# Dense products moved between the visits and the waits of a head pair, and the first attention head's loads in two queues

## The chip, the cores and the metric

The kernel runs on one core of a Trainium2 chip. The metric is the device time of one execution in microseconds, given as the median of repeated runs. Beside it stands one profiled execution, from which all durations below are read. The engines are called TensorE (PE in the rows, its weight loads PEld), VectorE (DVE), ScalarE (ACT), GpSimd (POOL) and SyncE (SP); ACTq and SPq are the queues from which ScalarE and SyncE start transfers.

## What is computed

One layer of a hybrid model over 128 prompt tokens and 512 latent tokens, T = 640 in all, of width 1024. It mixes differential attention (4 heads) with a bidirectional RWKV-7 scan (8 heads of 64), gates the two, and ends in a convolutional gated MLP. The outputs are both token groups, the new keys and values and the final scan states.

```python
h = x * (1 + sc1) + sh1
proj = h @ p['w_in']
q, k, v, rw, gates = jnp.split(proj, [...])          # 3 * 512 | 1792 | 2048 columns
o_att = diff_attention(apply_rope(q), [apply_rope(k), k_ctx], [v, v_ctx], lam)   # latents; the prompt has no rotary
# RWKV, for both directions d, token after token:
sa = jnp.einsum('bhvk,bhk->bhv', S, a_t)
S = S * w_t[:, :, None, :] + sa[..., None] * b_t[:, :, None, :] + v_t[..., None] * k_t[:, :, None, :]
y = jnp.einsum('bhvk,bhk->bhv', S, r_t)
...
o_rw = (y_rw * g_rw) @ p['w_o_rwkv']
mix = (ga * (o_att @ p['w_o_attn']) + gb * o_rw) @ p['w_out']
x = layer_norm(ALPHA * x + g1 * mix, ...)
# then ConvGLU: w_up, a 3-tap convolution, gelu(u) * val, w_down, a second layer norm
```

## The kernel before

Everything keeps features on the 128 partitions and tokens along the free axis, in two halves of 320 (HALF). The program runs in stages: modulation and the first input columns (up to some 70 us), the mixer (to 687 us), the attention (to about 787 us), the output projections and the MLP. The change lies in the mixer and at the first head of the attention.

**Dense products.** All columns of `w_in` are computed by `dense_steps` (L215): for each of 8 blocks of the inner dimension and each half of the tokens, three matrix products (high part by high part, high by low, low by high) in one PSUM bank. `load_w` brings a slab of four weight blocks in (L183, SyncE's queue), casts it on ScalarE (L186, `wh`) and subtracts on GpSimd (L187, `wl`). There are three buffers each for `ws`, `wh` and `wl`. A finished half is evacuated by ScalarE: into `raw` for the RWKV columns, into `vt` at L937 for the values, into `tg` at L1009 for the gates.

**The flow.** These products, with the work of `rw_a` (the RWKV projections of a head pair), `values`, `qk_head` and `gate`, form one long generator, `flow`. `pull(n)` takes its next n products and writes them into the program at the place of the call; `need(i, key)` pulls until a named input of pair i is there. `behind(n, f)` puts a function f after the next n products of the flow: the transposes of the values (L944) and of the keys (L981, L982) stand behind 14. TensorE's order is the order in which the program is written here, so each `pull(n)` fixes how many dense products stand at its place.

**A head pair.** The eight RWKV heads go in four pairs, i = 0 to 3. The recurrence is done in 10 chunks of 64 tokens for each of the two directions. The steps of a pair:

- `rw_c` (L644) multiplies AR by BK for all chunks; VectorE masks the results into MS (L651).
- `rw_i` inverts the 32 x 32 triangles on VectorE: four transposes (L704), each followed by `side()` and `pull(8)`; then 30 rounds of substitution (L711 to L713), each with `pull(4)`; then two transposes into Y11 (L722), four back into MS, and `pull(56)`. Beside it run generators kept in `sides`: `rw_d` (transposes of BK and values) and, for i > 0, `rw_f(i - 1)`, the normalization and gating of the pair before (L888 to L914), whose last instruction stores `yr`.
- `rw_m` completes the inverse in two small multiplications (L735, L743) with an evacuation between them by ScalarE (L737, `Vt`) and a `pull(12)`. Then come ten **visits**, v = 0 to 9. A visit has, as far as it exists, four transposes of a group of chunks (`turned`, L766), `joined` of the group before (L802 to L820), `solved` of its own group (L781), a sequential `step` of the states (L828, L830), then `side(3)` and `pull(10)`. The results of `solved` are copied to QQ (L788) and UV (L793) by VectorE and ScalarE; the next visit's `joined` reads them at L802 and L805. In the visits of pairs 0 to 2 the side generator is `rw_b(i + 1)`, which prepares the next pair's AR, BK and decays on VectorE and GpSimd.
- `rw_e` reads out the outputs (L869, evacuated by ScalarE at L870) and transposes the final states (L876).

The main loop (L1025 to L1047) goes through the pairs: `rw_e(i - 1)`, `need(i, "v_in")`, `rw_c(i)`, `rw_i(i)`, `rw_m(i)`. After `rw_f(3)` the rest of the flow is pulled without a pause.

**The attention's first head.** `load_head` (L1083 to L1094) brings queries and keys of one head from `qk_dram` with twelve transfers (L1090), then the values. `attend` starts with the scores (L1109). The loads of head 0 are written after the mixer, but the scheduler places them on SyncE's queue among the last of the mixer's transfers.

Of the kernel before, what the change touches and what calls it, by code (L numbers as in the profile page):

```python
# [11 lines left out]
F32 = mybir.dt.float32  # L12
# [54 lines left out]
def tile_layer(ctx, tc, x_prompt, x_sample, cache_k, cache_v, state_rwkv, c, c_ctx, w_ada, b_ada, w_in,  # L67
# [4 lines left out]
    nc = tc.nc  # L72
# [364 lines left out]
    def behind(n, f):  # L437

        later.append([n, f])
# [257 lines left out]
    def rw_i(i):  # L697
        MS = R[i]["MS"]

        X = rp.tile([P, 32, 32], F32, name="X", tag="st")  # L700
        tmp = rp.tile([P, 256], F32, name="tmpx", tag="tmpx")
        turns = [(X[32 * g:32 * g + 32], MS[32 * (g // 2):32 * (g // 2) + 32, 8 * (g % 2):8 * (g % 2) + 32, 32 * (g // 2):32 * (g // 2) + 32].rearrange("p c t -> p t c")) for g in range(4)]
        for x, m in turns:
            nc.vector.transpose(out=x, in_=m)  # L704
            side()
            pull(8)
        nc.vector.memset(X.rearrange("p t s -> p (t s)")[:, ::33], 1.0)
        for j in range(1, 31):
            n = 31 - j
            tv = tmp[:, 0:j * n].rearrange("p (t r) -> p t r", r=j)  # L710
            nc.vector.tensor_tensor(out=tv, in0=X[:, j:j + 1, 0:j].broadcast_to([P, n, j]),  # L711
                                    in1=X[:, j + 1:32, j:j + 1].broadcast_to([P, n, j]), op=ALU.mult)
            nc.vector.tensor_tensor(out=X[:, j + 1:32, 0:j], in0=X[:, j + 1:32, 0:j], in1=tv, op=ALU.add)  # L713
            side()
            pull(4)
        while "d_in" not in R[i]:
            side()
            pull(4)

        Y11 = rp.tile([32, 32, 40], F32, name="Y11", tag="bk", bufs=2)  # L720
        for g in range(2):
            nc.vector.transpose(out=Y11[:, :, 8 * g:8 * g + 32], in_=X[32 * g:32 * g + 32].rearrange("p t s -> p s t"))  # L722
        R[i].update(Y11=Y11)
        for x, m in turns[2:] + turns[:2]:
            nc.vector.transpose(out=m, in_=x)
        pull(56)

    def rw_m(i):
        AR, BT, UV, gs, st_in, MS = (R[i][k] for k in ("AR", "BT", "UV", "gs", "st_in", "MS"))
# [6 lines left out]
        for g in range(4):  # L736
            nc.scalar.copy(  # L737
                out=Vt[32:64, g::4, :], in_=ps[32 * g:32 * g + 32, 0:320].rearrange("p (c s) -> p c s", s=32))
        pull(12)
        ps = bank(psR, "m", 2)  # L740
        for ix in range(40):
            g, sl = ix % 4, ix // 4
# [89 lines left out]
        for v in range(10):  # L832
            put = turned(v + 1) if 0 < v < 4 else None
            if v == 0:
                turned(0)()
                pull(10)
                put = turned(1)
            if 1 <= v <= 5:
                joined(v - 1)
            if v < 5:  # L840
                solved(v)
            if put:
                put()
            if v > 2:
                s = v - 3
                step([(d, cc, ST[:, d, cc + 1 - 2 * d, :]) for d, cc in ((0, 2 + s), (1, 9 - s))] +
                     ([(0, 1, FS[0]), (1, 0, FS[1])] if v == 7 else []))
            side(3)
            pull(10)
        R[i].update(UV=UV, ST=ST, FS=FS)  # L850

    def rw_e(i):
# [79 lines left out]
    def values(n4):  # L932
        vt = fl.tile([P, T], F32, name="vt", tag="o", bufs=OB)
        new = newx()

        def evac(cols, pd, bias):
            nc.scalar.activation(out=vt[:, cols], in_=pd, func=AF.Identity, bias=bias)  # L937

        def turned():
            vs = fl.tile([P, 5, P], F32, name="vs", tag="o", bufs=OB)  # L940
            for z0, nz in ((0, 4), (4, 1)):
                ps = new()
                for z in range(nz):
                    pq(nc.tensor.transpose(out=ps[:, z * P:(z + 1) * P], in_=vt[:, (z0 + z) * P:(z0 + z + 1) * P], identity=ident))  # L944
                nc.vector.tensor_copy(out=vs[:, z0:z0 + nz, :], in_=ps[:, 0:nz * P].rearrange("p (b n) -> p b n", n=P))
            AQ.dma_start(out=v_dram[n4].rearrange("b p n -> p b n"), in_=vs)
            AQ.dma_start(out=new_v[:, n4 * P:(n4 + 1) * P], in_=vs[:, 0, :])

        yield from project_in(load_w(w_in[:, 1024 + n4 * P:1024 + (n4 + 1) * P], KB), evac, new=new)
        behind(14, turned)  # L950

    def qk(h, col, out, scale, new):
        w = load_w(w_in[:, col:col + P], KB)
# [48 lines left out]
    qk_dram = tc.dram_tile([2, 4, 2, P, T + P], F32, name="qk_dram")  # L1002
# [22 lines left out]
    for i in range(4):  # L1025
        if i:
            rw_e(i - 1)
        else:
            pull(40)
        need(i, "v_in")  # L1030
        sides.append(rw_d(i))
        rw_c(i)
        if i:
            sides.append(rw_f(i - 1))
        rw_i(i)
        if i < 3:
            need(i + 1, "rk_in")
            sides.append(rw_b(i + 1))
        else:
            pull(10)  # L1040
        rw_m(i)
        while sides:
            side()
            pull(3)
# [38 lines left out]
    def load_head(h):  # L1083
        qs, kh, kl = [], [], []
        for m in range(2):
            rows = slice(64 * m, 64 * m + 64)
            for lst, nm, w, z, ys, nb in ((qs, "qs", T, 0, (0, 1), QSB), (kh, "ks", T + P, 1, (0, 0), 2 * QSB), (kl, "ks", T + P, 1, (1, 1), 2 * QSB)):
                t_ = ap_.tile([P, w], F32R, name=nm, tag=nm, bufs=nb)
                for y in range(2):
                    nc.sync.dma_start(out=t_[64 * y:64 * y + 64, :].bitcast(F32), in_=qk_dram[z, h, ys[y], rows, 0:w])  # L1090
                lst.append(t_)
        V = ap_.tile([P, 6, P], F32, name="V", tag="V", bufs=2)
        nc.sync.dma_start(out=V[:, 0:5, :], in_=v_dram[h].rearrange("b p n -> p b n"))
# [514 lines left out]
```

## Time and profile before

| | |
|---|---|
| median of 3 runs | 1409.14 us (1409.0 to 1413.62) |
| profiled execution, its own time | 1415.6 us |
| span of the profiled execution | 1413.6 us |
| TensorE busy | 1254.3 us, 89% of the span |
| VectorE busy | 960.7 us, 68% |
| GpSimd, ScalarE busy | 553.4 and 544.0 us, 39% and 38% |
| mean granted clock of TensorE | 0.941 of full speed |
| moved by DMA | 144.57 MB, mean 102 GB/s |

How the rows of the trace are read. In the page's list of groups a row names line, engine, operation, output and inputs and the number of instructions; behind the first bar stand their busy time in us and the mean of one in ns, behind the second the engine's idle time before them and what ended most of it. In the busy time by stretches, a row gives the stretch (us from the start of the span) and its length, the busy time of each engine with the number of instructions in brackets, then the granted clock of TensorE (1.00 is 2.4 GHz, 0.50 is 1.2 GHz), the busy share of the DMA engines and the GB/s moved; a share over 1 means that more transfers were under way than there are engines. In the order of time, a row gives start, duration, engine, line, operation, output and inputs, the number of consecutive instructions merged in the row, and in square brackets how long the engine was idle before it and what it had waited for.

### The profile page before, as it was taken

The page shows a single profiled execution, that of the slowest core. Times are in us where ns is not written, and L with a number is a line of the kernel's source. Part 1 is how long each engine was busy: PE and PEld are TensorE (multiplying, and loading weights), DVE is VectorE, ACT ScalarE, POOL GpSimd, SP SyncE. Part 2 cuts the span into 40 slices and gives each one's busy share as a digit, 9 for nine tenths or more (in the row PEclk, how much of TensorE's full clock was granted, in tenths as well). Part 3 has the DMA queues.
Part 4 walks back from the last instruction along what each step waited for, and adds up shares of the span by engine and source line. Part 5 has one row for each costly group of instructions (what it writes and reads, how often), then busy time and mean ns, then how long its engine had stood idle before and what let it go on. Part 6 is the DMA issues. An engine that isn't in the chain of part 4 may idle for free. (4 is left out here: it accounts for less than half of the span.)

```text
span 1413.6 us, 26568 instructions
## 1 busy us (share of the span) xinstructions
PE 1254.3 (89%) x10583; PEld 1118.5 (79%) x10583; DVE 960.7 (68%) x1672; ACT 544.0 (38%) x1122; POOL 553.4 (39%) x415
## 2 busy tenths in 40 slices
PE   6989878887879899999888989969999999999995
PEld 5888777786768788889777777758988988989984
DVE  2367948896868667931366433687997987768778
ACT  3444333333333334232355321464443433434440
POOL 2244225432542232212220244546644635635631
PEclk9989979988998899989889999999999999999998
DMA  9412112221221111212666888423232231322222
GB/s 308 129 41 65 53 58 61 65 75 54 63 72 61 50 34 51 85 50 76 189 183 216 267 259 266 136 72 93 81 106 68 75 97 58 99 69 76 75 75 82
DMA packets 157455, 144.57 MB, mean 102 GB/s; under 512 B 10490, under 2 KB 128020, under 8 KB 157332
## 3 DMA queue, kind: packets, MB, share of 16 engines
q1 hardware_dynamic: 147490, 127.85, 29.6%
q10 hardware_dynamic: 9842, 15.03, 3.1%
q8 instruction: 83, 1.36, 0.4%
q14 instruction: 40, 0.33, 0.1%
HBM read 121.06 MB, written 19.69 MB: 100 GB/s over the span
## 5 line engine op out<-in xcount | busy, mean ns | idle before, releaser
L187 POOL TENSOR_TENSOR wl<-ws,wh 128x512 fp32r<-128x512 f32 x100 | 139.1, 1393 | 393.2 <-ACT wh L186 361.6
L224 POOL TENSOR_TENSOR wl<-sums,wh 128x512 fp32r<-128x512 f32 x88 | 137.0, 1562 | 39.4 <-ACT wh L223 35.7
L1431 PE MATMUL ps_d<-oph,wh 128*128 128x320 f32 x440 | 137.6, 313 | 11.6 <-DVE u L1443 5.2
L224 POOL TENSOR_TENSOR wl<-wu,wh 128x512 fp32r<-128x512 f32 x63 | 88.8, 1409 | 142.6 <-ACT wh L223 129.2
L1431 PE MATMUL ps_d<-oph,wl 128*128 128x320 f32 x440 | 137.0, 311 | 1.2 <-POOL wl L224 1.2
L1431 PE MATMUL ps_d<-opl,wh 128*128 128x320 f32 x440 | 136.5, 310 | 1.1 <-DVE opl L224 1.1
L186 ACT CAST wh<-ws 128x512 fp32r<-128x512 f32 x100 | 61.6, 618 | 136.7 <-PE ps_d L215 37.2
L215 PE MATMUL ps_d<-hh,wl 128*128 128x320 f32 (+1 forms) x304 | 102.8, 338 | 0.0
L215 PE MATMUL ps_x<-hh,wl 128*128 128x320 f32 (+1 forms) x304 | 101.6, 334 | 0.6 <-POOL wl L187 0.6
L215 PE MATMUL ps_d<-hl,wh 128*128 128x320 f32 (+1 forms) x304 | 102.0, 335 | 0.0
L215 PE MATMUL ps_x<-hh,wh 128*128 128x320 f32 (+1 forms) x304 | 101.8, 335 | 0.0
L215 PE MATMUL ps_d<-hh,wh 128*128 128x320 f32 (+1 forms) x304 | 101.6, 334 | 0.0
L215 PE MATMUL ps_x<-hl,wh 128*128 128x320 f32 (+1 forms) x304 | 101.2, 333 | 0.0
L1431 PEld LDWEIGHTS ps_d<-oph,wh 128*128 128x128 f32 x440 | 83.0, 189 | 16.0 <-ACT wh L223 9.1
L1431 PEld LDWEIGHTS ps_d<-opl,wh 128*128 128x128 f32 x440 | 83.0, 189 | 2.3 <-POOL hf L1346 1.3
L1431 PEld LDWEIGHTS ps_d<-oph,wl 128*128 128x128 f32 x440 | 83.1, 189 | 1.9 <-POOL wl L224 1.7
L223 ACT CAST wh<-sums 128x512 fp32r<-128x512 f32 x88 | 54.6, 620 | 64.7 <-PE ps_e L1431 25.2
L1465 PE MATMUL acc<-wh,gh 128*128 128x512 f32 x185 | 73.6, 398 | 2.6 <-ACT gh L223 2.6
L1466 PE MATMUL acc<-wl,gh 128*128 128x512 f32 x185 | 73.4, 397 | 0.0
L1467 PE MATMUL acc<-wh,gl 128*128 128x512 f32 x185 | 72.3, 397 | 0.5 <-DVE gl L224 0.5
L223 ACT CAST wh<-wu 128x512 fp32r<-128x512 f32 x63 | 39.1, 621 | 73.3 <-PE acc L1467 30.1
L215 PEld LDWEIGHTS ps_d<-hh,wl 128*128 128x128 f32 x304 | 61.9, 203 | 2.0
(430 smaller groups left out, 3649.7 us busy)
## 6 DMA issues: line engine op xcount, KB each, us to landing
wu<-in_w_up_dram SPq DMA_DIRECT2D x42, 512.0 KB
ws<-in_w_in_dram SPq DMA_DIRECT2D x76, 256.0 KB
wa<-in_w_ada_dram SPq DMA_DIRECT2D x24, 512.0 KB
ws<-in_w_down_dram SPq DMA_DIRECT2D x44, 256.0 KB
wa<-in_w_ada_dram SPq DMA_DIRECT2D x8, 1024.0 KB
ks<-qk_dram SPq DMA_DIRECT2D x32, 192.0 KB
g_dram<-tg ACTq DMA_DIRECT2D x16, 320.0 KB
tg<-g_dram SPq DMA_DIRECT2D x16, 320.0 KB
```

The costliest lines, as they stand in the source:

```text
L186: nc.scalar.copy(out=wh, in_=ws)
L187: (lo_eng or nc.gpsimd).tensor_tensor(out=wl, in0=ws, in1=wh.bitcast(F32), op=ALU.subtract)
L215: pq(nc.tensor.matmul(pd, w[:, k, :], x[:, g, sl], start=g == 0 and z == 0, stop=g == kb - 1 and z == 2))
L223: nc.scalar.copy(out=hi, in_=src)
L224: (lo_eng or nc.vector).tensor_tensor(out=lo, in0=src, in1=hi.bitcast(F32), op=ALU.subtract)
L1431: nc.tensor.matmul(ps, w[:, k, :], x[:, b, k, :], start=k == 0 and z == 0, stop=k == 3 and z == 2)
L1465: nc.tensor.matmul(acc, a_h, wh, start=first, stop=False)
L1466: nc.tensor.matmul(acc, a_h, wl, start=False, stop=False)
L1467: nc.tensor.matmul(acc, a_l, wh, start=False, stop=last)
```

## The change

Seven edits. In `rw_i` the four transposes of pairs 1 to 3 are followed by 12 products each instead of 8, and 72 instead of 56 stand at the end for pairs 1 and 2. Between the two multiplications of `rw_m` stand 18 instead of 12. The visits 1 to 5 get 5 products instead of 10. After `rw_e(i - 1)`, ahead of pairs 1 and 2, 16 products are new. The transposes of the values go behind 20 products instead of 14. Half of the twelve loads of the first attention head, those of the partitions 64 to 127, are started by ScalarE instead of SyncE. Lines from 1028 on have a number higher by one after the change.

```diff
@@ rw_i
         for x, m in turns:
             nc.vector.transpose(out=x, in_=m)
             side()
-            pull(8)
+            pull(12 if i else 8)
...
         for x, m in turns[2:] + turns[:2]:
             nc.vector.transpose(out=m, in_=x)
-        pull(56)
+        pull(72 if 0 < i < 3 else 56)
@@ rw_m
-        pull(12)
+        pull(18)
         ps = bank(psR, "m", 2)
...
             side(3)
-            pull(10)
+            pull(5 if 0 < v < 6 else 10)
@@ values
-        behind(14, turned)
+        behind(20, turned)
@@ main loop
         if i:
             rw_e(i - 1)
+            pull(16 if i < 3 else 0)
         else:
             pull(40)
@@ load_head
                 for y in range(2):
-                    nc.sync.dma_start(out=t_[64 * y:64 * y + 64, :].bitcast(F32), in_=qk_dram[z, h, ys[y], rows, 0:w])
+                    (nc.scalar if y and not h else nc.sync).dma_start(out=t_[64 * y:64 * y + 64, :].bitcast(F32), in_=qk_dram[z, h, ys[y], rows, 0:w])
```

How the order of the instructions changes is shown at three places. A row is line, operation, output and inputs, shape, and the number of instructions merged in it. First TensorE between `rw_e(0)` and `rw_c(1)`, before (L869 and L876 are `rw_e`, L644 is `rw_c`):

```order
L869 MATMUL ps_m<-AR_2160,ST 64x64 x2
L869 MATMUL ps_m<-AR_2161,ST 64x64 x2
L869 MATMUL ps_m<-AR_2160,ST 64x64 x2
L876 MATMUL ps_m<-ident,ST 64x128 x2
L644 MATMUL ps_m<-AR_3705,BK_3707 128x128
L644 MATMUL ps_ch<-AR_3705,BK_3707 128x128
```

and after, the last rows of the same place (L215 is a dense product, L981 and L982 are the transposes of a key tile):

```order
L215 MATMUL ps_d<-hh,wl 128x322
L215 MATMUL ps_d<-hh,wh 128x320
L215 MATMUL ps_d<-hl,wh 128x320
L981 MATMUL ps_x<-ident,ck 128x128
L982 MATMUL ps_x<-ident,qkt 128x128
L644 MATMUL ps_m<-AR_3775,BK_3777 128x128
L644 MATMUL ps_ch<-AR_3775,BK_3777 128x128
```

Sixteen products now stand between L876 and the first product of the next pair, where there were none. The second place is TensorE in a visit of pair 3, between the step of the states (L828) and the next `joined` (L802), before:

```order
L828 MATMUL ps_ch<-ST,AR_5248 64x64 x2
L215 MATMUL ps_x<-hh,wh 128x322
L215 MATMUL ps_x<-hl,wh 128x322
L215 MATMUL ps_x<-hh,wl 128x322
L215 MATMUL ps_x<-hh,wh 128x322
L215 MATMUL ps_x<-hl,wh 128x322
L215 MATMUL ps_x<-hh,wl 128x322
L215 MATMUL ps_x<-hh,wh 128x320
L215 MATMUL ps_x<-hl,wh 128x320
L215 MATMUL ps_x<-hh,wl 128x320
L215 MATMUL ps_x<-hh,wh 128x320
L802 MATMUL ps_m<-BT,QQ 64x64 x2
```

and after:

```order
L828 MATMUL ps_ch<-ST,AR_5328 64x64 x2
L215 MATMUL ps_d<-hh,wl 128x320
L215 MATMUL ps_d<-hh,wh 128x322
L215 MATMUL ps_d<-hl,wh 128x322
L215 MATMUL ps_d<-hh,wl 128x322
L215 MATMUL ps_d<-hh,wh 128x322
L802 MATMUL ps_m<-BT,QQ 64x64 x2
```

Ten products there have become five. The third place is SyncE's queue at the end of the mixer (L183 are weight slabs, here those of the next stage, L914 is the store of `yr`, L1090 and L1091 are the loads of queries and keys), before:

```order
L183 DMA ws<-in_w_in_dram 128x4x128 x3
L183 DMA ws<-in_w_o_rwkv_dram 128x4x128 x2
L914 DMA yr_dram<-yc 128x640
L183 DMA ws<-in_w_o_rwkv_dram 128x4x128
L1090 DMA qs<-qk_dram 64x640 x2
L1090 DMA ks<-qk_dram 64x768 x4
L1090 DMA qs<-qk_dram 64x640 x2
L1090 DMA ks<-qk_dram 64x768 x4
L1093 DMA V<-v_dram 128x5x128
```

and after:

```order
L183 DMA ws<-in_w_o_rwkv_dram 128x4x128 x4
L914 DMA yr_dram<-yc 128x640
L1091 DMA qs<-qk_dram 64x640
L1091 DMA ks<-qk_dram 64x768 x2
L1091 DMA qs<-qk_dram 64x640
L1091 DMA ks<-qk_dram 64x768 x2
L1094 DMA V<-v_dram 128x5x128
```

Six of the twelve loads have left this queue, and four slabs of the next stage stand ahead of them instead of three. ScalarE's own order there, after (L1009 are evacuations of the last gate, L1012 is its store, L1115 is the first softmax):

```order
L1068 DMA lq<-in_da_lambda_dram 1x256
L1091 DMA qs<-qk_dram 64x640
L1091 DMA ks<-qk_dram 64x768
L1009 ACTIVATE tg<-ps_d,bs 128x128
L1009 ACTIVATE tg<-ps_d,bs 128x192
L1009 ACTIVATE tg<-ps_d,bs 128x320
L1073 ACTIVATE ls<-ls 1x2
L1091 DMA ks<-qk_dram 64x768
L1012 DMA g_dram<-tg 128x640
L1091 DMA qs<-qk_dram 64x640
L1091 DMA ks<-qk_dram 64x768 x2
L1115 ACTIVATE pt,zz<-S,mx 128x128
```

The six loads that moved stand here, two ahead of the last gate's evacuations and four behind them.

## Rows read from the trace of the kernel before

**Rows 1.** The page: busy time of the engines, then two groups of instructions

```profile
PE 1254.3 (89%) x10583; PEld 1118.5 (79%) x10583; DVE 960.7 (68%) x1672; ACT 544.0 (38%) x1122; POOL 553.4 (39%) x415
...
L187 POOL TENSOR_TENSOR wl<-ws,wh 128x512 fp32r<-128x512 f32 x100 | 139.1, 1393 | 393.2 <-ACT wh L186 361.6
...
L186 ACT CAST wh<-ws 128x512 fp32r<-128x512 f32 x100 | 61.6, 618 | 136.7 <-PE ps_d L215 37.2
```

**Rows 2.** Stretches: busy PE, PEld, DVE, ACT, POOL (count), clock, DMA share, GB/s

```profile
127.90:175.30 47.40, 40.04 (x320) 37.88 (x321) 45.40 (x84) 18.02 (x36) 10.91 (x9) 0.94 0.19 54
186.20:232.00 45.80, 41.55 (x560) 36.96 (x561) 22.61 (x55) 17.03 (x38) 16.83 (x13) 0.85 0.16 47
232.00:249.40 17.40, 14.87 (x236) 13.21 (x234) 16.98 (x25) 6.85 (x16) 14.52 (x11) 1.00 0.26 82
267.40:324.20 56.80, 46.48 (x360) 43.44 (x358) 54.06 (x95) 21.36 (x43) 19.90 (x16) 0.90 0.23 70
549.50:598.20 48.70, 44.87 (x418) 42.05 (x420) 46.59 (x83) 16.09 (x34) 12.74 (x9) 1.00 0.25 79
607.20:640.00 32.80, 32.80 (x531) 29.72 (x532) 11.77 (x37) 11.78 (x29) 3.82 (x3) 0.91 0.13 37
```

**Rows 3.** Stretches, the dense products (L215) alone: PE, PEld, clock, DMA share, GB/s

```profile
674.60:687.00 12.40, 12.40 (x82) 12.19 (x82) 1.00 0.72 214
325.30:329.00 3.70, 3.58 (x12) 3.18 (x12) 0.50 0.00 0
```

**Rows 4.** In order of time, TensorE's waits (in brackets) between pairs and in solves

```profile
255.57 0.58 PE L644 MATMUL ps_m<-AR,BK 64*128 64x128 f32 x1 [3.60 <-DVE MS L651]
...
324.19 1.04 PE L735 MATMUL ps_m<-Y,MS 32*32 32x32 f32 x52 [3.38 <-DVE Y L722]
...
398.57 0.55 PE L644 MATMUL ps_m<-AR,BK 64*128 64x128 f32 x1 [5.52 <-ACT y L870]
...
559.55 0.66 PE L680 MATMUL ps_m<-ident,BK 128*128 128x128 f32 x4 [1.46 <-ACT sd L890]
...
602.93 0.75 PE L743 MATMUL ps_m<-MS,Vt 32*32 32x32 f32 x4 [2.37 <-ACT Vt L737]
```

**Rows 5.** In order of time: TensorE and ScalarE in one visit of pair 3

```profile
617.99 0.28 PE L781 MATMUL ps_ch<-UV,MS 64*64 64x64 f32 x4
...
619.14 0.37 ACT L788 COPY QQ<-ps_ch 64x256 f32<-64x256 f32 x1
...
619.78 0.60 PE L766 MATMUL ps_m<-ident,AR 128*64 128x128 f32 x4
```

**Rows 6.** TensorE's waits in pair 0's visits, then a stretch among them

```profile
200.59 0.29 PE L802 MATMUL ps_m<-BT,QQ 64*64 64x64 f32 x2 [1.09 <-ACT qkh L223]
201.75 0.27 PE L802 MATMUL ps_m<-BT,QQ 64*64 64x64 f32 x1 [0.87 <-ACT QQ L788]
...
225.60 0.27 PE L802 MATMUL ps_m<-BT,QQ 64*64 64x64 f32 x1 [1.01 <-ACT QQ L788]
...
203.30:213.60 10.30, 9.68 (x70) 8.73 (x66) 2.65 (x7) 2.98 (x6) 1.28 (x1) 0.50 0.06 23
```

**Rows 7.** In order of time: TensorE's waits at the transposes of the values

```profile
109.38 0.44 PE L944 MATMUL ps_x<-ident,vt 128*128 128x128 f32 x2 [0.96 <-ACT vt L937]
...
111.04 0.81 PE L944 MATMUL ps_x<-ident,vt 128*128 128x128 f32 x3 [1.23 <-ACT vt L937]
```

**Rows 8.** The first head's loads on SyncE's queue, the first scores, their stretch

```profile
678.89 1.14 SPq L1090 DMA_DIRECT2D qs<-qk_dram  x2
...
684.54 2.51 SPq L1090 DMA_DIRECT2D ks<-qk_dram  x4
...
689.93 0.93 PE L1109 MATMUL S<-ks,qs 128*128 128x64 f32 x5 [1.94 <-DMA ks<-qk_dram]
691.61 0.60 PE L1109 MATMUL S<-ks,qs 128*128 128x64 f32 x2 [0.74 <-DMA ks<-qk_dram]
...
683.00:693.00 10.00, 6.75 (x42) 6.09 (x41) 1.14 (x5) 3.01 (x8) 2.56 (x2) 0.92 1.05 275
```

## The prediction

> **What bounds the kernel now.** I read the page's first section, then the busy time by stretches, then the waits of TensorE. TensorE is busy 89% of the span [rows 1], more than any other engine, so the question is where its idle time lies. In the mixer two kinds of stretch alternate, four times each [rows 2]. In the solve of a pair (`rw_i`) VectorE is the limit: busy 45.4 of 47.4 us, 54.1 of 56.8 and 46.6 of 48.7 in pairs 0, 1 and 3, while TensorE has 4 to 10 us to spare. In the visits of `rw_m`, VectorE is busy about half of the time or less (22.6 of 45.8 us, 11.8 of 32.8) and TensorE sets the pace; in pair 3 it has no idle time at all. A third stretch, the last visits and `rw_e`, is VectorE's again where the next pair is being prepared beside it (17.0 of 17.4 us after pair 0). So products in the visits cost time, and products in the solve's waits should be free. That is what the change trades.
>
> **The price of a product.** The last 12.4 us of the flow, where TensorE does little else, hold 82 products: 0.15 us each at the full clock [rows 3]. At the 1.2 GHz level, twelve took 3.58 us, 0.30 each.
>
> **The change part by part.** The order of TensorE's instructions gives the counts. The visits 1 to 5 of the four pairs lose 100 products (15.0 us of TensorE). The waits gain 136 (20.4 us): 48 between the transposes of pairs 1 to 3, 32 at the ends of the solves of pairs 1 and 2, 24 before the second multiplication of `rw_m` (L743), 32 after `rw_e` ahead of pairs 1 and 2. The 36 in excess (5.4 us) come out of the tail of the flow, after the last `rw_f`, where 82 become 46. The work is the same, so the sum is made over idle time.
>
> *Filled waits: -20.4 us, less what isn't covered.* The waits at those places are longer than what is put into them [rows 4]: 3.60 and 5.52 us before L644 against 2.4 each (16 products), 3.38 us before L735 at the end of pair 1's solve, pair 2 alike, against 2.4 each, 2.37 us before L743 in pair 3 against 0.9 (6 products; pairs 0 and 2 are alike). The transposes come at the head of the solve, where what TensorE loses is taken back at its later waits on VectorE. Not covered: the six products before L743 in pair 1, where TensorE didn't wait (0.9), and about half of the sixteen in pair 3's solve (1.2 of 2.4): there the only waits before L735 are near 1.2 us, the longest 1.46 us [rows 4], and L735 itself didn't wait. With 0.9 for waits that move, 3.0 is uncovered. Bounds: 0, and 8 if the two waits before L644 travel with TensorE's own lateness instead of shrinking (4.8 more). I take 3.0, since the waits of rows 4 are on VectorE and ScalarE: **-17.4**.
>
> *The visits' lost cover: +4.3 us.* Between `solved` (L781) and the next `joined` (L802), the QQ and UV copies must run on ScalarE and VectorE, and the dense products and four transposes cover them. In pair 3, without disturbance, L781 ended at 618.27, the last QQ copy at 619.51, the transposes at 620.38 [rows 5]: TensorE came 0.87 us late, and five products are 0.75, so that visit stays covered by a hair. Worked out in the same way for the sixteen `joined` that follow a shortened visit: ten have 0.75 us or more in hand, three have 0.42 to 0.65 and will wait 0.5 us together, and three wait already, because ScalarE stood in a cast of the flow or VectorE was late [rows 6]; these lose the full 0.75. Sum 2.8. Of the four steps after visit 5 two have nothing in hand: 1.5 more. Bounds: 0 if the waits' causes move away with the flow's phase, 15.0 if all twenty lose their cover. 4.3 is nearest the undisturbed pattern.
>
> *Values' transposes behind 20 products instead of 14: -1.0 us.* TensorE waited 0.96 and 1.23 us for ScalarE's evacuation before such transposes [rows 7]; six products (0.9) go ahead of them, in a stretch that isn't VectorE's. Bounds 0 and -1.8; the last such block waits 5 us too, but inside pair 0's solve, where it is free.
>
> *The attention's start: +3.2 us.* TensorE arrived there at 687.1 and then waited 1.94 and 0.74 us for the last keys [rows 8]. With 36 products fewer after the last `rw_f` it comes 5.4 us sooner relative to that `rw_f`; what the loads don't gain becomes wait. Before, SP issued the twelve loads from 678.89 to 687.05, 0.6 us each; the last landed some 4.5 us later (691.6). After, SP's six start behind the fourth slab of the next stage. Its buffer comes free once TensorE has done the flow's last tile but one (just before the last `rw_f` product) and the first slab has had its cast and subtraction, 0.6 and 1.4 us [rows 1]; with SP's two issues ahead of the loads this is near 3 us after the last `rw_f` product, against 4.3 before. ScalarE's six stand among its evacuations of the flow's last products, four of them behind these. With the flow's last product at 6.9 us after that `rw_f` product, an evacuation of 0.5, the four issues (2.5) and the gate's store (0.3), the last load is issued near 10.2, against 12.4 before. So the keys come 2.2 us sooner, TensorE 5.4: 3.2 us more wait. Bounds: 0.3 (both the 1.3 us of the earlier start and the 3.8 us of six issues are gained) and 5.4 (nothing is). What is queued behind the loads on ScalarE is the first softmax, which needs them anyhow.
>
> The DMA engines were full while these loads ran (share 1.05 from 683 to 693 us) [rows 8], which speaks against any gain from a second queue beyond the start. The Trainium skill, "DMA: Bandwidth & Descriptors", section "Issuing engines are not separate DMA queues", says that transfers started by different engines share the same 16 DMA engines and that a second issuer saves only the issue time. By that rule the row's full engines decide, and the 2.2 us shrink to the 1.3 of the earlier start.
>
> *The clock: -1.0 us.* After the 3.38 us wait of pair 1 twelve products ran at 1.2 GHz, 1.8 us more than at 2.4 [rows 3, 4]; with the wait filled this is returned there, and perhaps in pair 2. Against it, a visit whose waits add up to 1.96 us was followed by 10.3 us at 1.2 GHz, with TensorE busy 9.7 of them [rows 6]: up to 4.8 us lost. Two visits that now wait 1.0 us will wait 1.75. Bounds -4 and +5; I take -1, since waits of 1.0 us have not been followed by a fall.
>
> *Sum:* -17.4 + 4.3 - 1.0 + 3.2 - 1.0 = **-11.9 us**. The profiled execution took 1415.6 us, its span 1413.6, some 6 us above the median of the three runs, 1409.14 (1409.0 to 1413.6). I take the difference from the median: **1397 us**.
>
> **The rivals.**
>
> *The cover is needed everywhere.* The flow's evacuations and casts fall differently after the shift and disturb all visits as they did the three of rows 6. Then 15.0 stands for 4.3: -1.2 us, 1408. For it: in pair 0 a cast in ScalarE's queue made TensorE wait 1.96 us in one visit. Against it: thirteen of sixteen visits weren't disturbed so far.
>
> *VectorE sets the pairs' period.* If the preparation of the next pair (`rw_b`, on VectorE and GpSimd beside the visits) and not TensorE decides when the next solve starts, shorter visits in pairs 0 to 2 only lengthen the wait after `rw_e`, and just pair 3 is shorter. The visits of pairs 0 to 2 give 3 x 3.75 - 4.1 = 7.2 us of the sum; without them it is -4.7 us, 1404. For it: VectorE is busy 17.0 of 17.4 us just after pair 0's visits [rows 2]. Against: it is half idle in the visits, and the preparation waits there for TensorE's turns.
>
> *The queue gives nothing.* The full DMA engines deliver the keys 1.3 us sooner, not 2.2, whoever issues them: -11.0 us, 1398. The place is the first scores of the attention.
>
> *Slower: the clock falls in the visits.* If the cover is gone as in the first rival and, on top, the clock falls after the two visits that wait 1.0 us now (1.75 then), this is -1.2 + 2 x 4.8 = +8.4 us, 1418. It decides where a visit's waits come near the 1.96 us of rows 6; all other visits stay below 0.8.
>
> **How the numbers follow.** Forecast 0.46; the queue rival 0.18; cover needed everywhere 0.16; VectorE's period 0.13; the clock 0.07. A measurement of this kernel tells about 0.5%, 7 us, from no change. Faster by more: forecast and queue rival, 0.64; within it: 0.29; slower by more: 0.07. The likeliest time is 1397 us. The low end, 1388, has nothing uncovered (-3.0), no new wait in the visits' steps (-1.5), two places of returned clock (-3) and an early key load (-1.5); the high end, 1408, takes in VectorE's period and most of the first rival.
>
> **What would show it.** Right: the waits before L735 in pairs 1 and 2 and before L644 in pair 2 shrink by 2 us or more each; the visits of pair 3 take about 3.5 us less than 32.8 at most places without TensorE idle; the wait before the first scores grows from 2.7 to 5 or 6 us; VectorE's share in the solves stays at 95%. Wrong: TensorE idle between L781 and L802 in ten or more visits; the solves longer, because VectorE waits for products that now come ahead of the `rw_f` ones; granted clock of 0.5 in the visits of pairs 2 and 3; or a slower attention stage, where the scheduler has also put loads and products in another order that I give no term, since its stretches show no single limit.

## The result, and the profile after

The change made the kernel slower: 1418.72 us as the median of 12 runs (1412.74 to 1425.88), against 1408.62 (1401.68 to 1413.62) before, a ratio of 1.0068 (95% interval 1.0048 to 1.0087). The prediction was 1397, with a range of 1388 to 1408.

The two profiled executions say less than the runs. The one of before (1415.6 us) lies above all 12 timed runs of before; the one of after (1412.74, span 1410.9) is the shortest of its 12. Both have a mean granted clock of about 0.94. Over the runs the clocks differ: after had 0.932 to 0.940, mean 0.937, and before, in 94 runs of it taken with the experiments, a mean of 0.9445, with 0.8 us of time for each 0.001 of clock (a line through those runs). By that line some 6 of the 10 us go with the clock and some 4 don't; by the line through the 12 runs of after (1.25 us for each 0.001) nearly all would, so this split is rough.

The mixer of after, from the first `rw_c` (L644) to the first scores, then pair 1 from its L735 to its first `solved`, then the solves of pairs 1 and 3 and the visits of pair 3, as busy time by stretches (columns as in [rows 2]):

```profile
111.10:691.10 580.00, 501.27 (x5878) 455.18 (x5877) 396.71 (x738) 206.63 (x448) 189.27 (x142) 0.91 0.21 64
...
321.10:347.40 26.30, 12.16 (x201) 10.12 (x200) 12.78 (x15) 7.23 (x16) 7.24 (x5) 0.68 0.22 68
...
263.20:321.10 57.90, 51.70 (x376) 48.41 (x375) 53.17 (x94) 21.79 (x43) 20.16 (x16) 0.91 0.23 69
...
556.90:610.10 53.20, 50.60 (x365) 47.49 (x363) 46.84 (x87) 17.34 (x38) 12.52 (x10) 0.90 0.24 77
620.80:652.00 31.20, 31.20 (x554) 27.76 (x553) 12.99 (x43) 9.57 (x24) 3.48 (x4) 1.00 0.16 48
```

The same mixer in the trace of before:

```profile
116.00:687.40 571.40, 499.34 (x5878) 453.50 (x5877) 394.03 (x734) 205.90 (x448) 188.21 (x140) 0.92 0.21 65
```

TensorE was idle for 580.00 - 501.27 = 78.7 us of the mixer. The waits were to be filled, and they aren't: before, it was 571.40 - 499.34 = 72.1. In pair 3 TensorE is now the busier engine of the solve (50.60 against 46.84), where VectorE was [rows 2]; its clock there is 0.90, where it was 1.00. The visits of pair 3 are as forecast: 31.2 us without any idle time, 3.8 less than the 35.0 before.

Where the idle time of after lies, in the order of time (waits of TensorE in brackets, as in [rows 4]):

```profile
257.12 0.37 PE L644 MATMUL ps_m<-AR,BK 64*128 64x128 f32 x1 [3.42 <-DVE MS L654]
...
330.51 0.64 PE L215 MATMUL ps_d<-hh,wh 128*128 128x322 f32 x1 [5.53 <-ACT qkt L956]
...
333.87 2.60 PE L743 MATMUL ps_m<-MS,Vt 32*32 32x32 f32 x80 [2.19 <-ACT Vt L737]
...
342.42 0.36 PE L755 MATMUL ps_m<-ident,st_in 64*128 64x64 f32 x1 [5.65 <-DVE ST L756]
...
411.75 0.49 PE L644 MATMUL ps_m<-AR,BK 64*128 64x128 f32 x1 [4.67 <-ACT y L870]
...
482.35 0.49 PE L735 MATMUL ps_m<-Y,MS 32*32 32x32 f32 x18
```

The waits before L735 are gone in pairs 1 and 2. In pair 1 three others stand behind it, 13.4 us together. Their origin is in ScalarE's rows there and in pair 2; a row from just ahead of pair 1 stands first:

```profile
243.88 0.72 ACT L223 CAST qkh<-qkt 128x640 fp32r<-128x640 f32 x1 [6.51 <-DVE qkt L964]
...
329.78 1.10 ACT L956 ACTIVATE qkt<-ps_d,bs 128x128 f32<-128x128 f32 x3 [12.97 <-DVE bs L246]
...
330.90 2.46 ACTq L961 DMA_DIRECT2D sw<-qkt  x4
333.41 1.30 ACT L737 COPY Vt<-ps_m 32x320 f32<-32x320 f32 x3 [2.03 <-DMA sw<-qkt]
...
487.49 0.68 ACT L1009 ACTIVATE tg<-ps_d,bs 128x128 f32<-128x128 f32 x2 [10.31 <-DVE bs L246]
```

A tile of the flow ends near the end of the solve. Its evacuation needs `bs`, two columns that VectorE takes out of PSUM (L246), and VectorE is in its transposes: ScalarE stands still for 12.97 us in pair 1 and 10.31 in pair 2, with `Vt` (L737), which the pair needs, queued behind; in pair 1 four transfers that ScalarE starts (L961, 2.46 us) stand ahead of `Vt` as well. TensorE waits too, since the next tile needs the bank. In pair 2 that isn't new: the trace of before has such a wait of 8.05 us there, ending at 476.14. In pair 1 it is; before, the evacuation came behind `Vt`. The first row shows the same at another place: ScalarE waits 6.51 us for the rotary work of VectorE (L964), the copy of `y` (L870) stands behind it, and TensorE waits 2.65 us for `y` before L644 of pair 1, where it waited 0.34 before, although 16 products were put there.

### The profile page after: what moved, and what is told of

The parts are those of the page before. It is cut to its first block, busy times and chain, and to the rows that moved or that the text cites. A ratio compares the mean times of both kernels' runs of the same rounds, so it can differ in the third digit from the quotient of the medians.

```text
span 1410.9 us, 26573 instructions
## 1 busy us (share of the span) xinstructions
PE 1251.5 (89%) x10583; PEld 1116.2 (79%) x10583; DVE 958.1 (68%) x1672; ACT 544.0 (39%) x1122; POOL 552.9 (39%) x415
## 5 line engine op out<-in xcount | busy, mean ns | idle before, releaser
L215 PE MATMUL ps_d<-hh,wh 128*128 128x320 f32 (+1 forms) x304 | 105.5, 347 | 8.4 <-ACT qkt L956 5.5
L215 PE MATMUL ps_d<-hh,wl 128*128 128x320 f32 (+1 forms) x304 | 104.9, 345 | 0.0
L215 PE MATMUL ps_d<-hl,wh 128*128 128x320 f32 (+1 forms) x304 | 103.3, 340 | 0.0
L215 PE MATMUL ps_x<-hh,wh 128*128 128x320 f32 (+1 forms) x304 | 99.8, 328 | 0.0
L215 PE MATMUL ps_x<-hh,wl 128*128 128x320 f32 (+1 forms) x304 | 99.3, 326 | 0.0
L215 PE MATMUL ps_x<-hl,wh 128*128 128x320 f32 (+1 forms) x304 | 98.5, 324 | 0.0
L215 PEld LDWEIGHTS ps_d<-hh,wh 128*128 128x128 f32 x304 | 64.2, 211 | 10.9 <-ACT qkt L956 5.8
```

Source lines behind the costliest of these rows:

```text
L215: pq(nc.tensor.matmul(pd, w[:, k, :], x[:, g, sl], start=g == 0 and z == 0, stop=g == kb - 1 and z == 2))
```

## The experiments

All ratios are against the kernel before on the same chip. The experiments ran on three chips, on which the median of before was 1407.7 to 1411.2 us; where two kernels ran on different ones, the difference of their ratios is given beside that of the medians. Theory A is what these rows show: tiles of the flow caught in the solves' ends. Theory B, later V, is that the shortened visits cost more than their cover, by TensorE's clock.

**The kernel before, again.**

> The kernel before, unchanged, a second time, for its spread and its granted clock. The profiled execution of before (1415.6 us, clock 0.941) lies above all its 12 timed runs (median 1408.6), and that of after (1412.7 us, clock 0.940) is the fastest of its 12 (median 1418.7). Theory A (what was lost is lost in the solves' ends, the clock is only noise on it): before's runs have the same mean clock as after's, 0.937 +- 0.003, and are shorter by 10 us at an equal clock. Theory B (what was lost is clock): before's runs have a clock of 0.943 or more, after's 12 had 0.932 to 0.940, and at an equal clock the two kernels take the same time.

1410.68 us, ratio 1.0012 (0.9992 to 1.0032), clocks 0.936 to 0.952, mean 0.944. Before has a higher clock than after (0.937), as B says; but at an equal clock after is still some 4 us longer by the line above, so A isn't excluded either. The profiled execution here took 1402.71, 13 us less than that of [rows 1] with the same program, 9.2 of them in the mixer, which has 69.6 us of idle time there.

**The solve as before.**

```diff
-            pull(12 if i else 8)
+            pull(8)
-        pull(72 if 0 < i < 3 else 56)
+        pull(56)
```

> The kernel after, with the products in the solve as before (8 behind each transpose, 56 at its end). Theory A (the added products bring a tile's end into the end of the solves of pairs 1 and 2, whose evacuation then stands ahead of Vt on ScalarE and waits for VectorE's transposes): the 12.97 and 10.31 us waits of ScalarE for bs before Vt are gone or below 4 us, L743 of pair 1 starts within 9 us of L735's start instead of 12.8, and the time is 1404 to 1411 us. Theory B (clock or lost cover in the visits, which this kernel keeps): 1416 to 1421 us.

1396.18 us, ratio 0.9921 (0.9892 to 0.9951): 22 us less than after (21 by the ratios), more than A said, and faster than before. In pair 1 the evacuation comes behind `Vt` again, with a wait of 4.61 us for `bs`, and L743 starts 8.9 us after L735's start instead of 12.8. In pair 2 the wait ahead of `Vt` is still there (11.23 us), against the expectation. So A's rows explain a part of the 22 us at most.

**`bs` by ScalarE, in after and in before.**

```diff
-                nc.vector.tensor_scalar(out=ev.bs, in0=pd[:, 0:2], scalar1=scale, scalar2=None, op0=ALU.mult)
+                nc.scalar.activation(out=ev.bs, in_=pd[:, 0:2], func=AF.Copy, scale=scale)
```

> The kernel after, with the two shift columns of a finished half (bs) taken out of PSUM by ScalarE instead of VectorE, so that the evacuation no longer waits for VectorE's transposes. Theory A: no wait of ScalarE for bs, L743 of pair 1 within 9 us of L735's start, pair 2 within 7, and 8 to 14 us less than after: 1404 to 1411 us. Theory B: within 3 us of after, 1416 to 1421 us; a few us more if the some 40 small instructions stand in ScalarE's way in the visits.

> The kernel before, with bs taken out of PSUM by ScalarE. Theory A (the 11 us that this gave to the kernel after are the two evacuations caught in the solves' ends, which before has in no such place): within 3 us of before's 1409. If ScalarE's waits for VectorE cost everywhere: 1400 us or less.

In after 1407.83 us, ratio 0.9983 (0.9961 to 1.0006), 11 less than after. In before 1403.66, ratio 0.9966 (0.9943 to 0.9989), 5 less, between its two branches. The traces put the two gains at different places. In after it is the end of pair 1's solve: from L735 to the first `solved` 15.5 us instead of 26.3, and L743 starts 4.3 us after L735's start. In before it is the time ahead of the first `rw_c`, which begins at 110.7 us instead of 116.0 and 115.7 in the two traces without the edit; its mixer took 566.8 us, against 571.4 and 562.2. So A holds for some 11 us, the evacuation caught in pair 1, and not for the 22 of the run above.

**`bs` by ScalarE and the solve as before, in after.**

> The kernel after with bs by ScalarE, and with the products in the solve as before (8 and 56). Theory A (what the added products in the solve cost is the evacuation in its end, and bs by ScalarE mends that): the same as either edit's better one, 1394 to 1398 us, no more than 3 us below the kernel with the solve as before (1396.2). If the products in the solve cost in themselves (TensorE is late for L735 in pairs 2 and 3), the gain over the kernel after with bs by ScalarE (1407.8) is again 8 us or more; if not, less than 3.

1396.58 us, ratio 0.9918 (0.9893 to 0.9942): 11 us less than with `bs` alone (9 by the ratios). By the time the second branch came true: with the short visits the products added to the solves cost more than they fill, with no evacuation in the way. Where they cost isn't shown: of the 17.2 us between the two traces 4.9 lie in the mixer and 11.0 behind the first scores, where both kernels do the same. That last stretch took 710 to 716 us in the three kernels with 126 or 182 products behind the last `rw_f` (this one, the one with the solve as before, and the next), and 718 to 727 in the other fifteen traces. So what is taken out of the tail of the flow is missed there, in a way that no run isolates.

**The visits alone, on before with `bs` by ScalarE.**

```diff
             side(3)
-            pull(10)
+            pull(5 if 0 < v < 6 else 10)
```

> The kernel before with bs by ScalarE, and the visits 1 to 5 with 5 products instead of 10; the 100 products go to the tail. Theory V (the shortened visits make TensorE's clock fall, in after 0.937 against 0.944): the clock falls from that of before with bs by ScalarE by 0.005 or more, mostly between the visits' start and rw_e, and the time grows by 4 (lost cover) + 6 to 8 (clock): 10 to 12 us over that kernel. If only the cover is lost, as predicted: 3 to 5 us over it, at the same clock.

1417.44 us, ratio 1.0061 (1.0038 to 1.0084): 13.8 us over the kernel without this edit, at a mean clock of 0.935 against 0.941. The stretch from the first `solved` to `rw_e` of pair 0 and the mixer, first with 10 products in the visits, then with 5:

```profile
189.10:237.70 48.60, 42.70 (x625) 37.86 (x624) 33.36 (x72) 20.37 (x47) 24.32 (x19) 0.99 0.21 67
...
110.70:677.50 566.80, 492.82 (x5878) 449.73 (x5877) 393.56 (x700) 213.92 (x483) 188.24 (x141) 0.91 0.21 65
```

```profile
189.50:244.20 54.70, 48.55 (x598) 43.26 (x597) 34.69 (x72) 17.65 (x38) 19.70 (x17) 0.77 0.13 39
...
111.10:703.50 592.40, 510.16 (x5877) 463.45 (x5876) 399.66 (x700) 214.50 (x481) 182.56 (x139) 0.89 0.22 66
```

In pair 0's visits, with 27 instructions fewer, TensorE is busy 5.9 us longer, at a granted clock of 0.77 instead of 0.99, and idle as long (6.2 us, against 5.9). Pair 1 is alike, at 0.77 instead of 0.93. So theory V holds there: the cover wasn't lost as idle time, but as clock. Over the mixer, at equal work, the 25.6 us more are 17.3 of busy time and 8.3 of idle time, half of it ahead of pair 1, where TensorE waits 4.4 us instead of 0.4; 12.3 of the 25.6 come back behind the first scores.

**All visits with 10 products, in after with `bs` by ScalarE, and in after alone.**

```diff
-            pull(5 if 0 < v < 6 else 10)
+            pull(10)
```

> The kernel after with bs by ScalarE, and all visits with 10 products. Theory V: the clock returns from 0.935 to 0.942 or more, and the time falls from 1407.8 by 6 to 10 us less what the 15 us of products cost that go back into the visits out of the tail (nothing in sum, since the tail gets shorter): 1398 to 1402 us. Without it: 1403 to 1408 at a clock of 0.935 to 0.938, since the visits' lost cover (4.3 by the prediction) is all that comes back.

> The kernel after with 10 products in all visits: the undoing of one edit alone. Theory V (the shortened visits lose cover, and the waits that follow make TensorE's clock fall): the clock returns from 0.937 to 0.943 or more and the time falls from 1418.7 by 15 to 25 us, to 1394 to 1404. If only the lost cover of the prediction comes back: 1412 to 1416 at a clock of 0.937 to 0.940.

With `bs` by ScalarE 1382.62 us, ratio 0.9818 (0.9784 to 0.9852), mean clock 0.951: 25.2 us less than with the short visits (23 by the ratios), where theory V had 6 to 10, and the fastest kernel of this study. In after alone 1391.17, ratio 0.9886 (0.9854 to 0.9917), clock 0.946: 27.5 us less than after (26 by the ratios), by the undoing of one line, where V had 15 to 25. The mixers of the two kernels with `bs` by ScalarE, with 5 and then with 10 products in the visits, and of after with 10:

```profile
112.00:681.80 569.80, 505.31 (x5878) 460.55 (x5877) 392.26 (x701) 212.82 (x482) 187.34 (x141) 0.90 0.22 65
```

```profile
112.10:659.40 547.30, 482.79 (x5878) 438.19 (x5877) 391.19 (x701) 214.38 (x483) 188.25 (x142) 0.94 0.23 69
```

```profile
111.10:669.50 558.40, 494.04 (x5877) 448.19 (x5877) 388.56 (x738) 208.61 (x450) 189.91 (x143) 0.92 0.22 68
```

With `bs` by ScalarE the mixers have the same 5878 instructions and in sum the same idle time (64.5 us in both), and TensorE is busy for 22.5 us less: in sum they differ by the clock. The waits lie elsewhere, though: the 8.1 us after `rw_e(0)` and `rw_e(1)` are gone, and the visits of pairs 0 and 1 have 9.9 more. In after itself most of what came back is idle time: 64.4 us instead of 78.7, with 7.2 less of busy time. It comes out of pair 1's solve and its end (12.4 us), the waits after `rw_e` (7.6) and pair 2's solve (4.4), while the visits and the wait before the first scores have 10.1 more. So the short visits cost at other places than the visits, too.

**Seven products in the visits, `bs` by ScalarE.**

> The kernel after with bs by ScalarE, and 7 products in the visits 1 to 5: between 5 (1407.8, clock 0.935) and 10 (1382.6, clock 0.951). A cost in proportion to the cover lost: 1396 to 1400 at 0.940 to 0.943. A threshold (two products give back 0.3 us of the 0.66 and 0.86 us waits before joined, and the clock no longer falls): 1388 or less at 0.948. A fall of the clock all the same: 1404 or more.

1399.69 us, ratio 0.9930 (0.9904 to 0.9957), clock 0.9385. The time is that of a cost in proportion, the clock lower than expected with it (0.940 to 0.943). Two products more are not enough to give all of it back.

**The solve as before, 10 products in the visits, `bs` by ScalarE.**

> The kernel after with bs by ScalarE, 10 products in all visits (1382.6 so far) and the products of the solve as before (8 and 56). If filling the solve's waits is worth what the prediction said, and only the shortened visits and the evacuation spoilt it: 7 to 12 us more than 1382.6, 1390 to 1395 (the 80 products, 12 us, go back to the tail). If the products in the solve cost as much as they save, as the 11 us between 1407.8 and 1396.6 with short visits say: 1372 to 1384.

1389.54 us, ratio 0.9857 (0.9824 to 0.9891): 6.9 more than 1382.6 (5.5 by the ratios, whose intervals overlap), just under the expected 7 to 12. Filling the solves with 80 products (12 us) is worth some 6 us when the visits are whole, hardly clear of the noise; with the short visits it cost some 10. Of the 8.6 us between the two traces 3.5 lie in the mixer and 5.4 behind the first scores.

**The second queue undone, in after, and in the fastest kernel.**

```diff
-                    (nc.scalar if y and not h else nc.sync).dma_start(...)
+                    nc.sync.dma_start(...)
```

> The kernel after, with all loads of the first head on SyncE's queue again. If the two queues brought nothing (the DMA engines are full): within 2 us of after's 1418.7. If they brought what the prediction took (the last key some 0.9 us sooner than by the earlier start alone): 1 to 3 us more than after. If they cost: 1413 to 1416 us.

> The kernel after with bs by ScalarE and 10 products in all visits (1382.6, the smallest spread so far), with all loads of the first head on SyncE's queue. Here TensorE waits for the keys of the first head with nothing else to do (2.45, 0.86 and 1.80 us). If the second queue brings the keys sooner: 1 to 4 us more than 1382.6. If the full DMA engines decide: within 1 us. If it costs: 1 to 3 us less.

In after 1421.81 us, ratio 1.0082 (1.0048 to 1.0115), which overlaps with after's. In the fastest kernel, whose runs are closest together, 1382.76 against 1382.62. From the end of the last `rw_f` product to the first scores it is 9.4 us with one queue and 9.2 with two, and to the transposes that end head 0 (L1147) 43.0 with one and 43.6 with two: the second queue is worth nothing.

**Products issued twice in the visits, `bs` by ScalarE, 5 products.**

```diff
+                        for t in range(twice[0]):
+                            pq(nc.tensor.matmul(pd, w[:, k, :], x[:, g, sl], start=... and t == 0, stop=... and t == twice[0] - 1))
...
+            twice[0] = 2 if 0 < v < 6 else 1
             pull(5 if 0 < v < 6 else 10)
+            twice[0] = 1
```

> The kernel after with bs by ScalarE, and each product in the visits 1 to 5 issued twice into the same sum: TensorE works there as with 10 products, while the flow stands where it does with 5. Those sums are then twice what they should be, so the outputs are not those of the reference; the time is what is asked. It adds 15 us of TensorE work that nothing gives back. If the cover and the clock in the visits are the cause (25.2 us): 15 more and 25 less, 1396 to 1402, clock 0.945 or more. If the flow's place is the cause: 1407.8 + 15 less the predicted 4.3 = 1417 to 1423.

1400.90 us, ratio 0.9963 (0.9944 to 0.9983), mean clock 0.948 against 0.935. TensorE does 15 us of work that nobody uses, and the kernel is no slower than without: 6.9 us less by the medians, 3 by the ratios, whose intervals overlap. So this work gives back some 18 to 22 us, near the 25 of the first branch. The visits of pair 0, with 5 products, and with the same 5 issued twice:

```profile
190.20:243.20 53.00, 48.80 (x598) 43.33 (x597) 32.58 (x72) 17.76 (x40) 19.31 (x17) 0.76 0.13 41
```

```profile
187.60:233.70 46.10, 42.91 (x624) 38.12 (x622) 29.97 (x71) 16.94 (x40) 19.70 (x15) 0.98 0.16 47
```

**The flow 25 products ahead, `bs` by ScalarE, 5 products.**

```diff
         else:
-            pull(40)
+            pull(65)
```

> The kernel after with bs by ScalarE, and 25 products more ahead of the first rw_c (65 instead of 40): the flow stands at rw_c(1) where it does with 10 products in the visits of pair 0, and the visits are as short as in after. The 25 products come out of the tail. If the flow's place is the cause: pair 1's solve takes 67 us as in the kernel with 10 products, instead of 75, and 6 to 10 us fall away: 1398 to 1402. If the visits themselves are the cause: 1406 to 1410, as without the shift (1407.8).

1397.11 us, ratio 0.9916 (0.9886 to 0.9946), clock 0.944: 10.7 less than without the shift (9 by the ratios), though the visits are as short. The place of the flow counts as well, and by the clock again: pair 1's solve (first L644 to L735) took 66.8 us with no stretch at 1.2 GHz, against 75.2 with 17 us of it. In pair 0's second visit TensorE didn't wait at all; later in those visits the clock still fell, for 10.2 us.

**The cast of a finished tile on GpSimd, in after and in the fastest kernel.**

```diff
-        split(hi, t_.bitcast(F32R), t_, nc.gpsimd)
+        nc.gpsimd.tensor_copy(out=hi, in_=t_)
+        nc.gpsimd.tensor_tensor(out=t_.bitcast(F32R), in0=t_, in1=hi.bitcast(F32), op=ALU.subtract)
```

> The kernel after, with the cast of a finished query or key tile (qkh) on GpSimd instead of ScalarE, so that it doesn't stand ahead of the copies of QQ and UV in the visits. If these waits (0.66 and 0.87 us in pair 0, 1.56 and 0.85 in pair 1) make the clock fall: both waits are gone or below 0.3 us, the stretches at 1.2 GHz in the visits of pairs 0 and 1 go from 17 to 25 us to below 7, and 1406 to 1411 us. If not: 1416 to 1420.

> The kernel after with bs by ScalarE, 10 products in all visits (1382.6) and the cast on GpSimd. With whole cover the cast costs one wait of 0.87 us in pair 0: 1380 to 1384, or slower by 1 to 4 us if GpSimd's queue delays the stores of the queries and keys or the weights' subtraction.

1424.10 us, ratio 1.0111 (1.0078 to 1.0145), and 1388.81, ratio 0.9856 (0.9826 to 0.9886): 5 and 6 us more than without it, with intervals that overlap those of the kernels without it. Nothing was gained, the expectation failed, and the rows say why. The first wait in pair 0's second visit of the former:

```profile
202.05 0.30 PE L802 MATMUL ps_m<-BT,QQ 64*64 64x64 f32 x2 [0.66 <-DVE QQ L788]
```

It is as long as with the cast on ScalarE. VectorE's own copy of QQ was late, behind the rotary products of the finished tile (L929, 1.73 us, and L964, 0.67 us), so ScalarE's cast, which the row of after names, was only the later of two. Whether the clock stays without these waits is therefore not tested.

## Why the prediction was wrong

Two steps failed: that the waits would be filled, and that the visits' products are worth only the cover that they give. Each edit was priced alone, and the edits don't add: undoing the visits' edit gave 27.5 us and undoing the solves' 22.5, where the whole change had lost 10.

**The filled waits, -17.4.** They weren't filled. Outside the visits, from `rw_c(0)` to the visits of pair 3, TensorE's idle time is 4.5 us longer than in the first trace of before and 6.7 longer than in the second. Three places show why.

- *Before L735 in pairs 1 and 2* the waits went, as forecast, and in pair 1 more came back behind them: the end of a tile, with its evacuation, had moved to where VectorE is busiest. That costs some 11 us. The prediction counted a product as 0.15 us of TensorE and nothing else. Each tile also brings an evacuation on ScalarE, `bs` and a token shift or a rotary turn on VectorE.
- *Before L644 of pair 1* [rows 4] was misread. The wait of 3.60 us lies inside `rw_c`, and no product of the change stands between the first product of `rw_c` and it. It is still there (3.42). In pair 2 5.52 became 4.67: it travelled, because ScalarE, ahead of the copy of `y`, waited for the weights of the next pair; and inside that `rw_c` 1.76 became 4.18. With the 2.65 us ahead of pair 1, the waits from `rw_e` to the end of `rw_c` of these two pairs went from 11.2 to 14.9 us, where the term has 4.8 less.
- *Pair 3's solve*: 1.2 us was to be uncovered there. L735 came 13.0 us later than in the first trace, while the solve had begun 7.5 later: 5.5 us for 16 products, more than their own 2.4. TensorE had become the bound of that solve, and its clock of 0.90 over 53.20 us means some 10 us at 1.2 GHz, where the solve of before had none; that is some 5 us.

The bounds of this term (nothing to 8 us uncovered) were too narrow. That waits can be filled is right by itself: in after with 10 products in all visits, the same products after `rw_e` and in the solves leave no wait from `rw_e` to the end of `rw_c` of pairs 1 and 2, and 12 us of products in the solves are worth some 6.

**The visits' lost cover, +4.3, and the clock, -1.0.** As idle time in the visits nothing was lost. The visits of the four pairs hold 13.9 us of it, against 15.4 before; of the sixteen `joined` behind a shortened visit two wait, 3.9 us together, as three did before; and the visits of pairs 2 and 3 gave up their 3.8 us each. The clock was wrong in size and in sign: the prediction looked for it after single waits, and only in one place gained and two lost. The shortened visits cost 13.8 us on before and 25.2 on after, both with `bs` by ScalarE, and 27.5 on after: in sum nearly all clock in the second case, two thirds of the mixer's loss in the first, one third in the last. The rest is idle time at other places.

What the clock costs can be read at equal work. In pair 0's visits (0.77 over 54.70 us, so some 25 at 1.2 GHz) TensorE was busy for 48.55 us, against 42.70 less 27 products of 0.15: 9.9 more. In the two mixers with `bs` by ScalarE (0.90 over 569.80 us and 0.94 over 547.30, so some 48 more at 1.2 GHz) it is 22.5 more. The Trainium skill, "TensorE: Matmul & The Clock Gate", section "Terms", puts the price of throttled time at that time times the share of the clock that is missing, here half. By that rule these are estimates of 12.6 and 24: the mixers agree, pair 0's visits cost a fifth less.

**The values' transposes, -1.0: right, and of no use.** The waits of [rows 7] are gone, and TensorE reached `rw_c(0)` 4.9 us sooner, where it then waited 4.18 us for VectorE; the fifth group of products there began at 121.2 us, against 120.9 before.

**The attention's start, +3.2: right in kind, too small.** TensorE came 10.8 us after the last `rw_f` product to the first scores, against 12.4, so 1.6 of the 5.4 us were gained, and 3.8 became wait:

```profile
691.07 0.27 PE L1110 MATMUL S<-ks,qs 128*128 128x64 f32 x1 [2.57 <-DMA ks<-qk_dram]
692.08 0.82 PE L1110 MATMUL S<-ks,qs 128*128 128x64 f32 x3 [0.74 <-DMA ks<-qk_dram]
```

Further waits follow (1.55 and 1.69 us, the latter for keys as well), and the transposes that end head 0 (L1147) came 45.4 us after that `rw_f` product, against 46.3 and 44.1 in the two traces of before (L1146): next to nothing of the 5.4 us was left.

The queue rival held: the second issuer is worth nothing (1382.76 against 1382.62). That agrees with the rule of the Trainium skill that the prediction set against the edit ("DMA: Bandwidth & Descriptors", section "Issuing engines are not separate DMA queues").

**The rivals.** The slower one, at 0.07, had one of the two mechanisms, the clock's fall, and the time (1418). The time is luck: its sum still has -17.4 for the filled waits, and it takes the cover to be gone everywhere, which it wasn't. "VectorE sets the pairs' period" wasn't tested alone. The wait ahead of pair 1, for `y` behind rotary work of VectorE, speaks for it there (2.65 us; 4.4 on before with `bs` by ScalarE and short visits; none in after with 10 products in all visits). Of the signs named, the waits before L735 and the visits of pair 3 came as forecast; the solves got longer, a sign of being wrong; idle time in ten or more visits, and the clock's fall in the visits of pairs 2 and 3, did not come in the trace of after.

What stays open is which arrangement makes the clock fall, and why the visits' and the solves' edits harm each other. Both more work in the visits and another place of the flow raise the clock. Waits go with it only loosely: pair 0's second `joined` had waits of 1.5 to 2.0 us in eight of the profiles, and the clock then fell for 10 to 20 us in five of them; with waits of up to 1.45 us it fell in one of ten. The program doesn't decide it alone: after and the kernel with one queue are the same up to the attention, and wait 1.53 us there both, but the visits of pair 0 then had a clock of 0.96 in the one profile and 0.77 in the other.

## What to carry to other kernels

A filler product isn't free because its engine waits: look up what it brings to the other queues (evacuation, small operations on the busiest engine), and where its tile ends. Wide products among narrow ones can be worth more than the waits that they cover: here they also kept TensorE's clock (0.98 against 0.76 in pair 0's visits, with the same products issued twice). Before taking them out, price the stretch at 1.2 GHz. A sum of edits, each priced alone, misses what one does to the place of the other's work. And compare two kernels by busy time at an equal count of instructions, and by the clocks of all runs, since one profile may be 7 us off.

## What was not expected of the hardware

TensorE at 1.2 GHz can stay there while it is busy nearly all the time. After two waits of 0.66 and 0.86 us, in after with `bs` by ScalarE:

```profile
201.50:222.00 20.50, 19.88 (x218) 17.89 (x216) 7.93 (x18) 5.25 (x11) 1.32 (x2) 0.50 0.10 33
```

It was busy 19.88 of 20.50 us there, with products 64 and 128 wide among the dense ones. And useless products cost nothing: with 15 us more work the kernel took 1400.90 us instead of 1407.83, 3 us less by the ratios, which is within the noise.
